# Half-size value pieces queued behind the steps of a recurrence, and one more value group moved among them

## The chip, the cores and the metric

The kernel runs on one core of a Trainium2 chip. The metric is the device time of one execution in microseconds (us), as the median of several runs. The engines named below are PE (TensorE, the matmul engine), DVE (VectorE), ACT (ScalarE), POOL (GpSimd) and SP (SyncE, which here issues nearly all transfers). A line number such as L516 is a line of the kernel before.

## The reference

A two-layer encoder trunk over 256 tokens of width 2048. Layer 0 mixes tokens by causal pooling, layer 1 by a recurrence (RWKV-7 style). Each mixer is followed by a gated feed-forward network of width 5632. What matters here is layer 1:

```
xr, xw, xk, xv, xa, xg = (h + xx * mu[j] for j in range(6))
r = xr @ w_r ;  k = xk @ w_k ;  v = xv @ w_v
g = sigmoid(xg @ g_la) @ g_lb
...
def step(state, inp):                    # per token, 32 heads of 64
    sa = einsum('bhvk,bhk->bhv', state, a_t)
    state = state * w_t + sa * b_t + v_t * k_t
    return state, einsum('bhvk,bhk->bhv', state, r_t)
...
return (normed(y) * g) @ w_o
```

The values `v` are a product of 256 x 2048 by 2048 x 2048, and each head needs only its own 64 columns of them.

## The kernel before, in words

Every float32 weight is split into a high and a low part (`split_weights`, L140): a transfer into a `raw` buffer, a cast on ACT into `wh` (L152), a subtraction on DVE into `wl` (L153). A product is then three matmuls. There are four `raw` buffers (`RAW`) and two each of `wh` and `wl` (`WB`).

The 2048 channels of layer 1 are worked in eight groups of 256 channels (four heads each). `values(gi)` (L504) makes the values of one group: four weight pieces of 512 KB, each with 24 matmuls of 256 columns (L515, L516, L517), 96 in all, accumulated in one PSUM bank and copied out by ACT (L520). Its left operands are the sixteen tiles `xv`, which are taken from a pool `mx` of forty tiles that other intermediates share.

The stages of layer 1 that matter follow each other like this:

- The values stage (L794): `values(0)` to `values(3)`, woven with the gate projections (`loras`, L711 to L713) and with `invert(0)`, a triangular inversion of small systems for groups 0 to 3, which is a long row of alternating products and sums on DVE (L633, L634). Its systems come back from DRAM (`dM`, L624) and its results go there (`dZ`, `dW`, L637, L639).
- A preparation stage (L1071): the first six of the sixteen remaining value pieces (`LV`), half of `prepare` for groups 4 to 7, and `ready(0)`, which loads one group's tiles (`KB`, `AR`, L832, L833), transposes them (L840), forms the gram tiles (L853, masked by DVE in L856) and completes the inverses (L875, L882).
- The recurrence (L1084): `all_chains()` advances the chains of the groups. A group's chain has twelve steps, four chunks of tokens with three products each (L907 and L910; L916; L921 and L925, then the state update on DVE in L930 or L932), with ACT copies between them (L912, L917, L937). A new group starts every eight steps (`STAG`), so one or two chains are alive, and there are 68 steps. Woven into these steps are the remaining ten value pieces (over steps 0 to 20, `VL`), the rest of `prepare`, `invert(1)`, `ready` of the later groups, `head_norm` with the gating (L958 to L960), and the output projection (`out_proj`, L1022 to L1024) from step 26 on.

The function `weave` (L432) only sets the order in which instructions are traced: after each step of its main generator, every other generator is advanced as far as it is due. The order on each engine is then made by a planner that simulates a timeline (L1162): it takes instructions as they become ready in the simulation, by priority, which is the traced order unless it is raised. The chain steps are raised by 30 (`HP`). A value matmul that is ready early can thus be placed long before the step it was traced in. `queued(name)` (L137) ties the instructions traced under it behind a recorded instruction on the same engine: they can be placed later than that one, not earlier. On the chip each engine works its list in order.

Of the kernel before, what the change touches and what calls it, by code (L numbers as in the profile page):

```python
# [10 lines left out]
F32 = mybir.dt.float32  # L11
# [24 lines left out]
HP, VL, HNL = 30, 20, 6  # L36
LV, LP, PE_, IE = 6, 14, 8, 16
# [55 lines left out]
def hybrid_encoder(ctx: ExitStack, tc: tile.TileContext, I, out):  # L93
# [156 lines left out]
    def ffn(layer, each=None):  # L250
        gcol = par[f"g2_{layer}"]
        with ExitStack() as st:
# [4 lines left out]
            rb = base[:, 4864:]  # L257
# [192 lines left out]
    def rwkv():  # L450
        with ExitStack() as st:
# [52 lines left out]
            def values(gi):  # L504
# [3 lines left out]
                for u in range(4):  # L508
                    (w, l), = split_weights(I["wv"][gi, u // 2][:, (u % 2) * 1024:(u % 2 + 1) * 1024])
                    for kk in range(4):  # L510
                        k = u * 4 + kk
                        cs = slice(kk * 256, (kk + 1) * 256)
                        for i in range(2):
                            xh, xl = xv[k][:, i * 128:(i + 1) * 128], xv[k][:, 256 + i * 128:256 + (i + 1) * 128]
                            nc.tensor.matmul(av[:, i], lhsT=xh, rhs=w[:, cs], start=(k == 0 and i == 0), stop=False, skip_group_check=True)  # L515
                            nc.tensor.matmul(av[:, i], lhsT=xh, rhs=l[:, cs], start=False, stop=False, skip_group_check=True)  # L516
                            nc.tensor.matmul(av[:, i], lhsT=xl, rhs=w[:, cs], start=False, stop=(k == 15), skip_group_check=True)  # L517
                    if u == 3:
                        vts[gi] = mx(F32, "vt") if gi < 4 else late[0].tile([128, 512], F32, name="vt", tag="vt", bufs=4)
                        nc.scalar.copy(vts[gi], acc)  # L520
                    yield
# [122 lines left out]
            with tc.tile_pool(name="rp1", bufs=1) as p1:  # L644
# [140 lines left out]
                for k in range(16):  # L785
# [8 lines left out]
                weave(chained(values(0), values(1), values(2), values(3)),  # L794
                      (loras(I["ga"], ("mu_g", "mu_g"), 128, (AF.Sigmoid, AF.Sigmoid), hid[2:]), 17, 0, 12),
                      (invert(0), 18, 0, 14))
# [90 lines left out]
            def chains(gi):  # L887
# [10 lines left out]
                for c in range(4):  # L898
# [5 lines left out]
                    with tc.high_priority(HP):  # L904
                        cb = cb_bank().rearrange("p (j x c) -> p j x c", j=2, x=2)
                        for jj, hc, u in heads_:
                            nc.tensor.matmul(cb[:, jj, 0, hc], lhsT=g_[jj][u % 2][k_, c], rhs=rows_of(u)[k_], start=(u == 0), stop=False, skip_group_check=True)  # L907
# [6 lines left out]
                    with tc.high_priority(HP):  # L914
                        for jj, hc, u in heads_:
                            nc.tensor.matmul(cb[b_, jj, 1, hc], lhsT=z[b_, u * 2 + i], rhs=rhs[b_, jj, hc], start=True, stop=True, skip_group_check=True)  # L916
                        nc.scalar.copy(two(vrow[b_]), cb[b_, :, 1])  # L917
                    yield
                    with tc.high_priority(HP):
                        for jj, hc, u in heads_:  # L920
                            nc.tensor.matmul(cb[k_, jj, 0, hc], lhsT=g_[jj][u % 2][b_, c, k_], rhs=rows_of(u)[b_], start=False, stop=True, skip_group_check=True)  # L921
# [244 lines left out]
```

## Time and profile before

| | us |
|---|---|
| median of 3 runs | 2184.95 |
| lowest and highest | 2180.51, 2186.39 |
| the profiled execution, its own time | 2181.9 |
| its span in the trace | 2180.1 |
| PE busy | 2116.9 (97% of the span) |
| DVE busy | 1553.9 (71%) |
| ACT busy | 1147.3 (53%) |
| mean granted PE clock | 0.981 |

The profile is one execution; times in it count from the span's start. "Busy" for PE counts overlapping, pipelined matmuls, so a full PE row does not mean that PE works at its peak. The granted clock is a share of full speed. In rows of stages the columns are the stage, its length, then for each engine the busy time with the number of instructions, then the granted clock, the mean busy share of the DMA engines and the GB/s that they moved. In rows of groups of instructions the last columns are the busy time, the mean duration in ns, and the idle time of the engine before them with what ended it. In rows of waits they are the total, the number of times and the longest. In rows of the timeline they are the start, the length, the engine and line, and in brackets the idle time before, with its releaser.

### The profile page before, as it was taken

How to read it: one execution, taken by the hardware profiler on the slowest of the kernel's cores; microseconds unless marked ns; L12 is line 12 of the kernel's file. 1: busy time of each engine (PE TensorE's matmuls, PEld its weight loads, DVE VectorE, ACT ScalarE, POOL GpSimd, SP SyncE). 2: the span in 40 equal slices, each digit the busy share in tenths (PEclk: the TensorE clock that was granted, in tenths of full speed). 3: DMA queues.
4: the chain of work that ended last, by engine and by line, in shares of the span. 5: the costliest groups of instructions: out<-in, count | busy, mean ns of one | idle time of the engine just before them, and what ended most of it. 6: DMA issues, size and time to landing. Idle time of an engine off the chain costs nothing.

```text
span 2180.1 us, 34748 instructions
## 1 busy us (share of the span) xinstructions
PE 2116.9 (97%) x13318; PEld 1843.5 (85%) x13318; DVE 1553.9 (71%) x2548; ACT 1147.3 (53%) x1884; POOL 30.6 (1%) x72
## 2 busy tenths in 40 slices
PE   7999999999999989999999999999999999999997
PEld 5888888888878879999988778788888888888786
DVE  8666666666787978688866767876666666677886
ACT  5544444444555478766745354554444444445444
POOL 0000000000000000011000000000000000000000
PEclk9999999999999999999998699999999999999999
DMA  6555565665566645466565343446666666655654
GB/s 232 174 187 191 186 191 187 190 187 190 196 198 217 207 155 163 163 210 207 171 218 151 108 121 105 160 121 191 188 189 189 188 189 189 188 191 199 204 202 156
DMA packets 147478, 395.11 MB, mean 181 GB/s; under 512 B 39280, under 2 KB 46832, under 8 KB 147056
## 3 DMA queue, kind: packets, MB, share of 16 engines
q1 hardware_dynamic: 146160, 390.80, 56.2%
q8 instruction: 104, 1.70, 0.3%
q10 hardware_dynamic: 1152, 2.10, 0.3%
q14 instruction: 62, 0.51, 0.1%
HBM read 376.59 MB, written 16.25 MB: 180 GB/s over the span
## 4 chain that ended last, share of the span: by engine, by line
PE 86%; DVE 6%; DMA 4%; ACT 2%; issue 1%; SPq 0%; ACTq 0%; DVEq 0%
PE acc L311 29%; PE acc L347 17%; PE acc L313 15%; PE acc L691 2%; PE acc L689 2%; PE acc L690 2%; DVE wl L153 2%; PE tp L347 2%; PE acc L1022 1%; PE acc L1024 1%; PE acc L1023 1%; DMA raw<-in_w 1%; PE acc L516 1%; PE acc L515 1%; PE cb L907 1%
## 5 line engine op out<-in xcount | busy, mean ns | idle before, releaser
L153 DVE TENSOR_TENSOR wl<-raw,wh 128x1024 fp32r<-128x1024 f32 (+1 forms) x525 | 640.2, 1220 | 432.2 <-ACT wh L152 428.0
L152 ACT CAST wh<-raw 128x1024 fp32r<-128x1024 f32 (+1 forms) x525 | 548.5, 1045 | 648.7 <-PE acc L311 276.9
L311 PE MATMUL acc<-xs,wh 128*128 128x512 f32 x2816 | 710.6, 393 | 3.7 <-DVE xs L266 3.2
L311 PEld LDWEIGHTS acc<-xs,wh 128*128 128x128 f32 x2816 | 504.9, 189 | 94.9 <-DVE xs L266 5.1
L313 PEld LDWEIGHTS acc<-xs,wl 128*128 128x128 f32 x2816 | 384.1, 190 | 27.5
L313 PE MATMUL acc<-xs,wl 128*128 128x256 f32 x2816 | 392.7, 282 | 0.0
L347 PE MATMUL acc<-vh,gT 128*128 128x512 f32 x640 | 184.9, 390 | 0.8 <-ACT vh L152 0.8
L347 PEld LDWEIGHTS acc<-vh,gT 128*128 128x128 f32 x640 | 119.7, 188 | 27.3 <-ACT vh L152 2.6
L691 PE MATMUL acc<-mx,wl 128*128 128x256 f32 x464 | 133.0, 287 | 3.5 <-DVE wl L153 3.5
L689 PE MATMUL acc<-mx,wh 128*128 128x256 f32 x464 | 132.1, 285 | 0.0
L690 PE MATMUL acc<-mx,wh 128*128 128x256 f32 x464 | 131.8, 284 | 0.0
L153 DVE TENSOR_TENSOR vl<-raw,vh 128x1024 fp32r<-128x1024 f32 x80 | 95.5, 1221 | 27.1 <-ACT vh L152 19.7
L347 PE MATMUL acc<-vl,gT 128*128 128x512 f32 x320 | 112.2, 389 | 0.0
L152 ACT CAST vh<-raw 128x1024 fp32r<-128x1024 f32 x80 | 80.9, 1050 | 49.3 <-PE acc L347 22.7
L355 ACT CAST vh<-T 128x1024 fp32r<-128x1024 f32 x56 | 58.9, 1052 | 80.5 <-DVE T L397 43.6
L347 PE MATMUL acc<-wh,gT 128*128 128x512 f32 x320 | 93.8, 390 | 0.7 <-ACT wh L152 0.7
L691 PEld LDWEIGHTS acc<-mx,wl 128*128 128x128 f32 x464 | 88.5, 191 | 5.3 <-DVE wl L153 5.2
L689 PEld LDWEIGHTS acc<-mx,wh 128*128 128x128 f32 x464 | 88.5, 191 | 0.8
L690 PEld LDWEIGHTS acc<-mx,wh 128*128 128x128 f32 x464 | 88.6, 191 | 0.0
L347 PE MATMUL acc<-vh,g 128*128 128x512 f32 x280 | 77.9, 391 | 1.1 <-ACT vh L355 0.6
L516 PE MATMUL acc<-wl,mx 128*128 128x256 f32 x256 | 74.2, 290 | 1.2 <-DVE wl L153 1.1
L515 PE MATMUL acc<-wh,mx 128*128 128x256 f32 x256 | 74.2, 290 | 0.0
(329 smaller groups left out, 3118.5 us busy)
## 6 DMA issues: line engine op xcount, KB each, us to landing
raw<-in_w SPq DMA_DIRECT2D x528, 512.0 KB, 4.4
raw<-in_wk SPq DMA_DIRECT2D x32, 512.0 KB, 3.7
raw<-in_wr SPq DMA_DIRECT2D x32, 512.0 KB, 3.7
raw<-in_wv SPq DMA_DIRECT2D x32, 512.0 KB, 4.0
raw<-in_wo SPq DMA_DIRECT2D x32, 512.0 KB, 3.6
raw<-in_pw SPq DMA_DIRECT2D x8, 512.0 KB, 7.8
dKB<-KB SPq DMA_DIRECT2D x16, 256.0 KB, 3.1
dKB<-AR SPq DMA_DIRECT2D x16, 256.0 KB, 3.7
```

The lines of the kernel that those rows point to most:

```text
L152: nc.scalar.copy(wh[:P, :step], raw[:P, :step])
L153: nc.vector.tensor_sub(wl[:P, :step], raw[:P, :step], wh[:P, :step].bitcast(F32))
L311: nc.tensor.matmul(acc, lhsT=w[:, cs], rhs=xs[q * 4 + kk], start=(q + kk == 0), stop=False, skip_group_check=True)
L313: nc.tensor.matmul(acc[:, :256], lhsT=l[:, cs], rhs=xs[q * 4 + kk][:, :256], start=False, stop=(q + kk == 6), skip_group_check=True)
L347: nc.tensor.matmul(out_, lhsT=lhsT, rhs=rhs, start=start, stop=stop, skip_group_check=True)
L355: nc.scalar.copy(wh, src)
L515: nc.tensor.matmul(av[:, i], lhsT=xh, rhs=w[:, cs], start=(k == 0 and i == 0), stop=False, skip_group_check=True)
L516: nc.tensor.matmul(av[:, i], lhsT=xh, rhs=l[:, cs], start=False, stop=False, skip_group_check=True)
L689: nc.tensor.matmul(acc[:, :256], lhsT=w[:, cs], rhs=xs[k][:, :256], start=(k == 0), stop=False)
L690: nc.tensor.matmul(acc[:, :256], lhsT=w[:, cs], rhs=xs[k][:, 256:], start=False, stop=False)
L691: nc.tensor.matmul(acc[:, :256], lhsT=l[:, cs], rhs=xs[k][:, :256], start=False, stop=(k == 15))
L907: nc.tensor.matmul(cb[:, jj, 0, hc], lhsT=g_[jj][u % 2][k_, c], rhs=rows_of(u)[k_], start=(u == 0), stop=False, skip_group_check=True)
```

## The change

- `values(gi)` hands back control after every second block of channels instead of every fourth: eight pieces of 12 matmuls a group instead of four of 24. The weight transfers and splits keep their size, one for two pieces.
- Once a chain has begun, the matmuls of each piece are traced under `queued("chain")`. The chain functions record each of their products of L907, L916 and L921 as `last["chain"]`, so a piece can't be placed ahead of the last such product of the step that it is traced behind.
- The values stage makes three groups (`VF = 3`) instead of four, and the gate projections and the inversion are due over 18 and 21 of its 24 half pieces (before: 12 and 14 of 16 pieces). The fourth group comes first among the remaining ones.
- Of the remaining 40 half pieces, 12 lie in the preparation stage (`LV`, one and a half groups as before) and 28 in steps 0 to 30 of the recurrence (before: 10 whole pieces in steps 0 to 20).
- `rb` names its 256 columns by both ends.

```
-HP, VL, HNL = 30, 20, 6
-LV, LP, PE_, IE = 6, 14, 8, 16
+HP, VL, HNL = 30, 30, 6
+VF, LV, LP, PE_, IE = 3, 12, 14, 8, 16
...
-            rb = base[:, 4864:]
+            rb = base[:, 4864:5120]
...
                     for kk in range(4):
                         k = u * 4 + kk
                         cs = slice(kk * 256, (kk + 1) * 256)
-                        for i in range(2):
-                            ... three matmuls
-                    if u == 3:
-                        vts[gi] = mx(F32, "vt") if gi < 4 else late[0].tile([128, 512], F32, name="vt", tag="vt", bufs=4)
-                        nc.scalar.copy(vts[gi], acc)
-                    yield
+                        with queued("chain") if "chain" in last else ExitStack():
+                            for i in range(2):
+                                ... the same three matmuls
+                        if k % 2 and k < 15:
+                            yield
+                vts[gi] = mx(F32, "vt") if gi < 4 else late[0].tile([128, 512], F32, name="vt", tag="vt", bufs=4)
+                nc.scalar.copy(vts[gi], acc)
+                yield
...
-                weave(chained(values(0), values(1), values(2), values(3)),
-                      (loras(I["ga"], ("mu_g", "mu_g"), 128, (AF.Sigmoid, AF.Sigmoid), hid[2:]), 17, 0, 12),
-                      (invert(0), 18, 0, 14))
+                weave(chained(*(values(g) for g in range(VF))),
+                      (loras(I["ga"], ("mu_g", "mu_g"), 128, (AF.Sigmoid, AF.Sigmoid), hid[2:]), 17, 0, 6 * VF),
+                      (invert(0), 18, 0, 7 * VF))
...
-                            nc.tensor.matmul(cb[:, jj, 0, hc], lhsT=g_[jj][u % 2][k_, c], ...
+                            last["chain"] = nc.tensor.matmul(cb[:, jj, 0, hc], lhsT=g_[jj][u % 2][k_, c], ...
...
-                            nc.tensor.matmul(cb[b_, jj, 1, hc], lhsT=z[b_, u * 2 + i], ...
+                            last["chain"] = nc.tensor.matmul(cb[b_, jj, 1, hc], lhsT=z[b_, u * 2 + i], ...
...
-                            nc.tensor.matmul(cb[k_, jj, 0, hc], lhsT=g_[jj][u % 2][b_, c, k_], ...
+                            last["chain"] = nc.tensor.matmul(cb[k_, jj, 0, hc], lhsT=g_[jj][u % 2][b_, c, k_], ...
...
-            vals = chained(*(values(g) for g in range(4, 8)))
+            vals = chained(*(values(g) for g in range(VF, 8)))
...
-            more += [(vals, 16 - LV, 0, VL), (prep, 28 - LP, 0, PE_), (invert(1), 18, PE_, IE), (reload(), 1, STAG + 12, STAG + 13)]
+            more += [(vals, 8 * (8 - VF) - LV, 0, VL), (prep, 28 - LP, 0, PE_), (invert(1), 18, PE_, IE), (reload(), 1, STAG + 12, STAG + 13)]
```

More of the change, by code (lines that the diff above doesn't have):

```diff
@@ L512, in values @@
                         cs = slice(kk * 256, (kk + 1) * 256)
-                        for i in range(2):
[L514 to L517, printed above, removed]
-                    if u == 3:
-                        vts[gi] = mx(F32, "vt") if gi < 4 else late[0].tile([128, 512], F32, name="vt", tag="vt", bufs=4)
-                        nc.scalar.copy(vts[gi], acc)
-                    yield
+                        with queued("chain") if "chain" in last else ExitStack():
+                            for i in range(2):
+                                xh, xl = xv[k][:, i * 128:(i + 1) * 128], xv[k][:, 256 + i * 128:256 + (i + 1) * 128]
+                                nc.tensor.matmul(av[:, i], lhsT=xh, rhs=w[:, cs], start=(k == 0 and i == 0), stop=False, skip_group_check=True)
+                                nc.tensor.matmul(av[:, i], lhsT=xh, rhs=l[:, cs], start=False, stop=False, skip_group_check=True)
+                                nc.tensor.matmul(av[:, i], lhsT=xl, rhs=w[:, cs], start=False, stop=(k == 15), skip_group_check=True)
+                        if k % 2 and k < 15:
[3 more added lines that the diff above has]
+                yield
             def placed(tile_, first):
@@ L906, in chains @@
                         for jj, hc, u in heads_:
-                            nc.tensor.matmul(cb[:, jj, 0, hc], lhsT=g_[jj][u % 2][k_, c], rhs=rows_of(u)[k_], start=(u == 0), stop=False, skip_group_check=True)
+                            last["chain"] = nc.tensor.matmul(cb[:, jj, 0, hc], lhsT=g_[jj][u % 2][k_, c], rhs=rows_of(u)[k_], start=(u == 0), stop=False, skip_group_check=True)
                         if c:
@@ L915, in chains @@
                         for jj, hc, u in heads_:
-                            nc.tensor.matmul(cb[b_, jj, 1, hc], lhsT=z[b_, u * 2 + i], rhs=rhs[b_, jj, hc], start=True, stop=True, skip_group_check=True)
+                            last["chain"] = nc.tensor.matmul(cb[b_, jj, 1, hc], lhsT=z[b_, u * 2 + i], rhs=rhs[b_, jj, hc], start=True, stop=True, skip_group_check=True)
                         nc.scalar.copy(two(vrow[b_]), cb[b_, :, 1])
@@ L920, in chains @@
                         for jj, hc, u in heads_:
-                            nc.tensor.matmul(cb[k_, jj, 0, hc], lhsT=g_[jj][u % 2][b_, c, k_], rhs=rows_of(u)[b_], start=False, stop=True, skip_group_check=True)
+                            last["chain"] = nc.tensor.matmul(cb[k_, jj, 0, hc], lhsT=g_[jj][u % 2][b_, c, k_], rhs=rows_of(u)[b_], start=False, stop=True, skip_group_check=True)
                         if c < 3:
```

## The prediction

> **What bounds the kernel now.** I read the page first: engine shares, and the clock by slices.
>
> ```profile
> span 2180.1 us, 34748 instructions
> ...
> PE 2116.9 (97%) x13318; PEld 1843.5 (85%) x13318; DVE 1553.9 (71%) x2548; ACT 1147.3 (53%) x1884; POOL 30.6 (1%) x72
> ...
> PEclk9999999999999999999998699999999999999999
> ```
>
> TensorE (PE) is busy almost throughout, at full granted clock but for one place: slices 21 and 22 (each 54.5 us) read 8 and 6. So I asked for busy time by stage around it: values with the gate projections (1020 to 1076), preparation (to 1111.5), the first recurrence steps with value work (to 1176), the steps after the value work is used up (to 1251.8), the rest of the recurrence (to 1411).
>
> ```profile
> core 0: us, PE busy (x) PEld busy (x) DVE busy (x) ACT busy (x) POOL busy (x), PEclk, DMA share, GB/s
> 1020.00:1076.00 56.00, 55.11 (x453) 54.29 (x453) 51.73 (x117) 35.65 (x67) 2.11 (x3) 1.00 0.52 165
> 1076.00:1111.50 35.50, 32.87 (x276) 30.86 (x276) 21.62 (x41) 22.41 (x41) 2.91 (x8) 0.95 0.74 228
> 1111.50:1176.00 64.50, 64.50 (x730) 58.01 (x728) 44.97 (x96) 35.30 (x78) 5.44 (x14) 1.00 0.56 182
> 1176.00:1251.80 75.80, 67.54 (x540) 56.30 (x541) 50.82 (x138) 28.74 (x68) 1.87 (x3) 0.66 0.40 116
> 1251.80:1411.00 159.20, 156.84 (x1403) 126.89 (x1402) 117.35 (x236) 81.53 (x171) 1.84 (x3) 0.98 0.40 126
> ```
>
> The first and third stages are limited by PE, with DVE close behind in the first (51.73 of 56). The fourth is the weak one: mean clock 0.66, and 75.80 - 67.54 = 8.3 us with no matmul at all. How the clock moves there is seen in windows of 2 us around each transition:
>
> ```profile
> 1182.00:1184.00 2.00, 1.91 (x18) 1.53 (x17) 0.00 (x0) 0.84 (x2) 0.00 (x0) 0.88 0.97 138
> ...
> 1216.00:1218.00 2.00, 2.00 (x7) 1.21 (x6) 1.86 (x5) 0.13 (x1) 0.76 (x1) 0.59 0.00 0
> ...
> 1234.00:1236.00 2.00, 1.78 (x13) 1.34 (x12) 1.23 (x2) 1.98 (x2) 0.00 (x0) 0.68 1.01 347
> ...
> 1250.00:1252.00 2.00, 2.00 (x6) 1.55 (x6) 0.33 (x1) 0.00 (x0) 0.00 (x0) 0.56 0.00 0
> ...
> 1282.00:1284.00 2.00, 0.96 (x5) 0.74 (x3) 1.66 (x4) 1.13 (x4) 0.00 (x0) 0.62 0.81 246
> ...
> 1288.00:1290.00 2.00, 2.00 (x11) 1.35 (x9) 0.69 (x1) 0.00 (x0) 0.00 (x0) 0.67 0.25 69
> ```
>
> Clocks are 1.00 or 0.50, so a mean gives the instant: 0.88 means a fall at 1183.5, 0.59 a rise at 1217.6, then fall 1234.7, rise 1251.8, fall 1282.5, rise 1289.3. The half-clock stretches last 34.1, 17.1 and 6.8 us. The first two, 51.2 us, cost up to 25.6 us of PE time; that is what is to be had.
>
> Where the value matmuls stand (one of their three lines, by the first three stages), and their spacing at full and, for the same shape in the gating, at half clock:
>
> ```profile
> 1020.00:1076.00 56.00, 33.72 (x118) 22.58 (x118) 1.00 0.52 165
> 1076.00:1111.50 35.50, 17.30 (x59) 11.45 (x58) 0.95 0.74 228
> 1111.50:1176.00 64.50, 23.23 (x80) 15.17 (x80) 1.00 0.56 182
> ...
> 1167.95 0.28 PE L517 MATMUL acc<-wh,mx 128*128 128x256 f32 x1
> ...
> 1169.14 0.28 PE L515 MATMUL acc<-wh,mx 128*128 128x256 f32 x1
> ...
> 1193.00 0.41 PE L960 MATMUL g<-hid,lbl 128*128 128x256 f32 x1
> ...
> 1194.92 0.41 PE L960 MATMUL g<-hid,lbl 128*128 128x256 f32 x1
> ...
> L516 PE MATMUL acc<-wl,mx x256: 274/283/415, 1020.6 to 1171.1; 128*128 128x256 f32 x128
> ```
>
> From 1167.95 to 1169.14 lie ten starts, 0.119 us each at full clock; from 1193.00 to 1194.92 nine, 0.213 us at half. With three lines, 3 x 80 = 240 value matmuls stand in the first recurrence stage; the last starts at 1171, so none is left for 1176 onward. Recurrence steps are dated by the chain's first product:
>
> ```profile
> L907 PE MATMUL cb<-vt,base x32: 214/272/320, 1111.6 to 1180.5; 64*128 64x64 f32 x32
> ...
> L907 PE MATMUL cb<-vt,G x96: 272/272/472, 1197.7 to 1385.3; 64*128 64x64 f32 x96
> ```
>
> Group 0 begins at 1111.6 (step 0); group 2, the first whose gram tiles are not in `base`, at 1197.7 (step 16): 86.1 / 16 = 5.4 us a step. The remaining 52 steps end about 1409, 4.1 us a step. So 1176 is step 12, and step 30 falls near 1255, just past the second half-clock stretch.
>
> **The change, part by part.** No arithmetic is added or removed: 768 value matmuls, 32 weight loads, 32 casts and 32 subtractions before and after. The edit of `rb` names the same 256 columns and costs nothing.
>
> *The fourth group leaves the values stage.* It is 96 matmuls, 96 x 0.119 = 11.4 us of PE, and four splits on DVE:
>
> ```profile
> L153 DVE TENSOR_TENSOR wl<-raw,wh 128x1024 fp32r<-128x1024 f32 x16 | 19.5, 1217 | 0.4 <-ACT wh L152 0.3
> ```
>
> 4 x 1.217 = 4.9 us. Since DVE stands at 51.73 of 56 with PE at 55.11, taking away 11.4 of PE and 4.9 of DVE leaves DVE first, near 47 of work. The inversion and gate projections are paced over 21 and 18 half pieces of 24, so their DVE work is packed, not cut. The saving lies between 4.9 (DVE) and 11.4 (PE); it is zero if the recurrence's start hangs on the transfers behind the inversion. I take 6, nearest to DVE.
>
> *The first steps hold fewer pieces.* A half piece is 12 matmuls, 1.43 us. By step 12, 13 of the 28 are due: 156 matmuls instead of 240. PE is busy 64.50 of 64.50 here, so 84 x 0.119 = 10.0 us come out, less where a chain's own latency shows instead. Bounds 0 and 10.0; I take 7, because PE is full throughout.
>
> *Steps 13 to 30 receive 15 pieces,* 180 matmuls: 21.4 us at full clock, 180 x 0.213 = 38.3 at half. There are 8.3 us of empty PE to absorb them, and the clock they may hold up. With s the share of the 51.2 us that is no longer at half clock, the stage changes by 38.3 - 16.9 s - 8.3 - 25.6 s = 30.0 - 42.5 s. Adding -6 and -7, the whole is 17.0 - 42.5 s, zero at s = 0.40.
>
> What s is depends on two falls. The first follows a stall that the change leaves:
>
> ```profile
> 1179.34 6.73 SPq L624 DMA_DIRECT2D sysM<-dM  x4
> ...
> DVE sysP L633 <- DMA sysM<-dM: 7.3, 1, 7.3
> ...
> PE cb L921 <- ACT sv L917: 4.0, 1, 4.0
> PE g L840 <- DMA KB<-dKB: 2.9, 3, 1.9
> ```
>
> DVE stands 7.3 us before the second inversion's first product, the head norms and state updates behind it wait, and PE runs dry for 4.0 us. Only the piece of the present step can fill that, so the first fall probably comes again. The rise is what I expect earlier. Compare the third stretch:
>
> ```profile
> 1283.16 0.80 PE L1022 MATMUL acc<-wh,ys 128*128 128x512 f32 x1 [1.04 <-DVE G L856]
> ...
> 1288.02 0.63 PE L1024 MATMUL acc<-wh,ys 128*128 128x512 f32 x1
> ```
>
> From 1283.16 on, full-width matmuls ran solid and the clock rose at 1289.3, two periods of 3.4 us after its fall; 3.4 us divides the other stretches too (10 and 5 times). In the first stretch such matmuls came only with the output projection. One piece at half clock is 12 x 0.213 = 2.6 us solid: alone a little short of a period, with gating or the next piece beside it enough. I take s = 0.65 in the first stretch and 0.8 in the second, whose fall came among chain products with little full-width work: (0.65 x 34.1 + 0.8 x 17.1) / 51.2 = 0.70. The sum is 17.0 - 29.8 = -12.8.
>
> The Trainium skill, "TensorE: Matmul & The Clock Gate", Part 1, puts this period at 3413 ns and has one busy period lift the clock; the trace agrees on the period. Its section "Why this matters for your kernels" asks for no idle gap above about 3 us. The second fall, with about 1 us idle before it, does not obey that: by that rule alone the second stretch would not be there, nor its 0.8 x 8.5 = 6.8 us to be won, and the sum would be -6.
>
> *Queues.* Value weights load on SP (0.33 us an issue); those behind the 6.73 us of L624 come late, and a late weight leaves its step's piece empty. Casts on ACT now wait for pieces that wait for chain steps, because only two `wh` buffers exist; behind such a cast stand the chain's copies. The nearest row:
>
> ```profile
> ACT wh L152 <- PE acc L1024: 4.9, 1, 4.9
> ```
>
> The DVE splits (7.5 x 1.217 = 9.1 us after 1176) fit beside 50.82 of 75.8. The sixteen `xv` tiles of the 40 `mx` stay until step 30 instead of 1171; a shortage would make the next group's KB loads late, and doubling today's 2.9 us of that wait costs 2.9. Two output-projection banks of three are wanted from step 26. For these I take zero, covered by the pieces themselves, with 4.9 + 2.9 = 7.8 as upper bound.
>
> The profiled execution took 2181.9 us (span 2180.1 and 1.8 around it), 3 below the median 2184.95. -12.8 gives 2169 against it and 2172 against the median; I say 2171.
>
> **Rivals.** *The moved work runs cold (slower).* The stall at 1180 drops the clock, and one piece a step never makes a solid period before the output projection does. Place: 1183 to 1217. Price: s = 0.2 gives 17.0 - 8.5 = +8.5, 2193; s = 0 gives +17, 2202. It decides below s = 0.40. For: the gating's twelve same-shaped matmuls from 1192.4 did not lift the clock, and PE records read nearly full there while it stayed 0.50. Against: a second such block in every step.
>
> *What leaves early is paid later (no change).* DVE and the inversion's transfers keep the start of the recurrence where it is (0 instead of -6), and at s = 0.55 the rest is -7 + 30.0 - 23.4 = -0.4: about 2183. For: DVE's 51.73 of 56. Against: the 4.9 us that DVE itself loses.
>
> *Nearly all is recovered (more gain).* Full PE savings, -11.4 - 10.0, and s = 0.9 give -21.4 + 30.0 - 38.2 = -29.6: about 2153. The first fall would have to vanish too; the 4.0 us gap speaks against it.
>
> *The order does not come out as written.* The queueing forbids a piece to go early, not late: if weights lag, pieces bunch at steps 20 to 30 beside the output projection, the first stretch stays cold and the second is cured, s = 17.1 / 51.2 = 0.33, +3.0, with 7.8 of queue waits +10.8: about 2195. Speaking for it: SP's 6.73 us.
>
> **How the numbers follow.** Forecast 0.50 (2160 to 2178); nearly all recovered 0.14; no change 0.18; cold 0.12; bunched 0.06. Runs of this kernel spread over 0.3%, so that is the bound for a difference. Faster 0.64, same 0.18, slower 0.18. The range 2151 to 2196 holds the recovered case's 2153 and reaches past the nearer slower ones, leaving out s = 0; it runs across both signs, but most of it is gain.
>
> **What would show it.** Value matmuls spread past 1230; the chain's first product some 5 us earlier than 1111.6; group 2's start about 13 us earlier than 1197.7 if the clock holds; one half-clock stretch below 15 us in place of 34.1, the second gone or short; PE-empty time in steps 13 to 30 below 8.3 us. Wrong, if the clock of these steps stays near 0.66 with 128x256 matmuls 0.21 us apart, if the values stage shortens by nothing, or if the chain's copies wait behind casts.

## The result, and the profile after

The changed kernel takes 2214.61 us (median of four runs, 2210.89 to 2217.57) against 2185.67 for the kernel before beside it: a ratio of 1.0134, with a 95% interval of 1.0109 to 1.0159. The forecast was 2171, so the sign was wrong. The profiled execution of the changed kernel has a span of 2209.1 us, 29.0 more than that of before. In its code the lines behind L515 stand one or two lower: the value matmuls are L516 to L518, the chain's first product is L909, the output projection L1024 to L1026.

First the page of the changed kernel:

```profile
span 2209.1 us, 34761 instructions
...
PE 2146.9 (97%) x13318; PEld 1866.5 (84%) x13318; DVE 1552.9 (70%) x2548; ACT 1147.1 (52%) x1884; POOL 29.4 (1%) x72
...
PEclk9999999999999999999868989999999999999999
```

The low clock is still there. Counted from 1, slices 20 to 22 and 24 read 8, 6, 8, 8, where before slices 22 and 23 read 8 and 6 (the prediction counts them from 0), so it begins two slices earlier. PE is "busy" 30 us longer with the same number of matmuls.

To see where the time went, both traces are cut at the same events: the last receptance product (before the values stage), the ends of groups 0, 2 and 6 (the square in `head_norm`, L980 before and L982 after; called here steps 12, 28 and 60, from which they are due; the first comes some 13 us behind the 1176 that the prediction calls step 12), and FFN 1's first matmul. Busy time by stage, the kernel before:

```profile
1019.80:1189.30 169.50, 162.07 (x1545) 151.48 (x1543) 122.89 (x263) 96.91 (x194) 11.57 (x27) 0.97 0.60 188
1189.30:1259.40 70.10, 65.75 (x549) 54.55 (x550) 51.67 (x134) 29.53 (x68) 1.37 (x2) 0.68 0.31 94
1259.40:1385.10 125.70, 123.85 (x1144) 100.34 (x1142) 87.59 (x174) 62.75 (x136) 1.23 (x2) 0.97 0.37 115
1385.10:1434.80 49.70, 47.19 (x260) 37.33 (x259) 44.32 (x95) 25.05 (x51) 0.00 (x0) 1.00 0.48 154
```

and the changed kernel:

```profile
1021.60:1192.00 170.40, 159.65 (x1331) 147.68 (x1330) 115.87 (x261) 86.79 (x184) 9.24 (x27) 0.80 0.52 161
1192.00:1263.10 71.10, 71.10 (x690) 61.60 (x691) 54.07 (x130) 35.41 (x73) 2.45 (x2) 0.97 0.43 135
1263.10:1415.20 152.10, 152.10 (x1229) 120.81 (x1225) 93.33 (x182) 67.57 (x142) 1.23 (x2) 0.94 0.36 111
1415.20:1464.70 49.50, 45.77 (x252) 37.48 (x251) 42.45 (x93) 24.76 (x52) 0.00 (x0) 0.97 0.43 135
```

The two stages up to step 28 together are only 1.9 us longer. In this pair of executions the whole loss, 26.4 us, stands in the third stage, in which no value matmul was to be moved. One of the three value lines in the first three of these stages, and one of the three output-projection lines in the last three; for each kernel the value rows come first:

```profile
1019.80:1189.30 169.50, 74.24 (x256) 0.97 0.60 188
...
1189.30:1259.40 70.10, 7.08 (x12) 0.68 0.31 94
1259.40:1385.10 125.70, 27.78 (x64) 0.97 0.37 115
1385.10:1434.80 49.70, 14.34 (x36) 1.00 0.48 154
```

```profile
1021.60:1192.00 170.40, 59.04 (x193) 0.80 0.52 161
1192.00:1263.10 71.10, 18.41 (x60) 0.97 0.43 135
1263.10:1415.20 152.10, 1.23 (x4) 0.94 0.36 111
...
1192.00:1263.10 71.10, 1.57 (x4) 0.97 0.43 135
1263.10:1415.20 152.10, 32.08 (x76) 0.94 0.36 111
1415.20:1464.70 49.50, 12.43 (x32) 0.97 0.43 135
```

From these rows comes a balance. The clock's loss is length times (1 - clock). A value matmul counts 0.119 us as in the prediction; one of the output projection counts 0.235, by four starts in the changed kernel's timeline, (1300.58 - 1299.64) / 4:

```profile
1299.64 0.39 PE L1026 MATMUL acc<-wh,ys 128*128 128x512 f32 x1
...
1300.58 0.39 PE L1024 MATMUL acc<-wh,ys 128*128 128x512 f32 x1
```

What is left over is called gaps: round trips, hand-overs, and the few small products that fall on the other side of a cut. The clock stands in the rows with two places, so the columns of clock and gaps hold to about 1 us. The balance says where the time stands, not what caused it.

| after minus before, us | length | clock's loss | values | output projection | gaps |
|---|---|---|---|---|---|
| to step 12 | +0.9 | +29.0 | -22.5 (-189) | 0 | -5.6 |
| steps 12 to 28 | +1.0 | -20.3 | +21.4 (+180) | -5.6 (-24) | +5.5 |
| steps 28 to 60 | +26.4 | +5.3 | +1.4 (+12) | +8.5 (+36) | +11.2 |
| to FFN 1 | -0.2 | +1.5 | 0 | -2.8 (-12) | +1.1 |
| sum | +28.1 | +15.5 | 0.3 | 0.1 | +12.2 |

The moved values were absorbed between steps 12 and 28, as forecast. Against the forecast, the place that they left got no shorter, and its clock fell; and the steps behind 28 got longer, where the output projection, which now starts 43 us later, stands with more gaps around it.

The first fall is seen in the changed kernel's timeline at the end of the preparation stage, and in windows of 2 and 20 us:

```profile
1087.93 0.28 PE L518 MATMUL acc<-wh,mx 128*128 128x256 f32 x1
1092.48 1.11 PE L842 MATMUL g<-base,KB 128*128 128x128 f32 x4 [4.27 <-DMA KB<-dKB]
```

```profile
1090.00:1092.00 2.00, 0.00 (x0) 0.00 (x0) 2.00 (x4) 0.73 (x2) 0.12 (x2) 0.73 0.76 182
...
1120.00:1140.00 20.00, 19.49 (x131) 17.29 (x132) 11.23 (x26) 9.48 (x24) 1.22 (x6) 0.50 0.47 155
```

PE ran out of value work at 1088 and waited 4.27 us for `KB`. The clock fell at 1090.9 (a mean of 0.73 in the first window) and, by the changes of the clock in the trace, came back at 1145.5: 54.6 us at half speed. In the kernel before the same wait was shorter, and value matmuls followed it at once:

```profile
1102.17 1.09 PE L840 MATMUL g<-base,KB 128*128 128x128 f32 x4 [2.37 <-DMA KB<-dKB]
1102.91 0.56 PE L515 MATMUL acc<-wh,mx 128*128 128x256 f32 x1
```

There the clock was down for 3.4 us.

### The profile page after: what moved, and what is told of

It reads as the page before. It is cut to its first block, busy times and chain, and to the rows that moved or that the text cites. A ratio compares the mean times of both kernels' runs of the same rounds, so it can differ in the third digit from the quotient of the medians.

```text
span 2209.1 us, 34761 instructions
## 1 busy us (share of the span) xinstructions
PE 2146.9 (97%) x13318; PEld 1866.5 (84%) x13318; DVE 1552.9 (70%) x2548; ACT 1147.1 (52%) x1884; POOL 29.4 (1%) x72
## 5 line engine op out<-in xcount | busy, mean ns | idle before, releaser
L516 PE MATMUL acc<-wh,mx 128*128 128x256 f32 x256 | 78.7, 307 | 0.0
```

## The experiments

Each ratio is to the kernel before on the same chip in the same job (its medians lay between 2179 and 2182 us there), with its 95% interval. The ratios are taken from all runs of a job; the ratio of the two medians can differ from them by up to 0.0024.

**The parts of the change.** The changed kernel without the queue:

```
-                        with queued("chain") if "chain" in last else ExitStack():
+                        with ExitStack():
```

> The changed kernel without the queueing alone: half pieces, three groups in the values stage, 28 pieces over 30 steps stay. Theory S (the queueing starves the start: value matmuls can no longer fill the wait for the KB transfers and the first steps, so the clock falls to half at 1091 and stays there for 54.6 us): the value matmuls run ahead again, the half-clock stretch at the start is gone or below 10 us, the time comes back to 2178 to 2192. Theory G (moving the fourth group costs, whatever the order on PE): it stays above 2205. Theory R (any new order made by the planner shifts the half-clock stretches by chance): anywhere between 2170 and 2215, with stretches in other places.

Measured: 2192.09 us, 1.0048 [1.0025, 1.0072]. Without the queue the planner pulls the values forward again (the last one at 1166 instead of 1265), the long fall at 1091 is gone, and some 19 of the 29 us with it; the time lies 0.1 us above the range of theory S and far below that of theory G.

The changed kernel with four groups in the values stage:

```
-VF, LV, LP, PE_, IE = 3, 12, 14, 8, 16
+VF, LV, LP, PE_, IE = 4, 12, 14, 8, 16
```

> The changed kernel with four groups in the values stage again (20 half pieces over 30 steps instead of 28), queueing and half size stay. Theory S: five and a half groups stand before the recurrence as in the kernel before, so the wait for the first KB transfer is filled and the fall at 1091 does not come at that place; the first steps still get one piece each, so part of the loss stays: 2190 to 2205, half-clock time before the feed-forward network between 61 and 92 us. Theory G: back to 2180 to 2188. Theory R: no order in it.

Measured: 2196.87 us, 1.0080 [1.0056, 1.0104], as theory S had it. In place of the long fall at 1091 stands one of 3.4 us at 1097, but up to step 12 there are still 51 us of half clock in all.

The queue alone, added to the kernel before with its whole pieces, four groups and twenty steps (the line that is added; the chain's products are recorded as in the change):

```
+                        with queued("chain") if "chain" in last else ExitStack():
```

> The kernel before with the queueing alone: whole pieces, four groups in the values stage, 10 pieces over 20 steps, each behind its chain step. Theory S: slower than before, 2190 to 2210, with more half-clock time in the steps 0 to 12 than the kernel before (3.4 us there). Theory G: within 0.3% of before, 2179 to 2192.

Measured: 2194.70 us, 1.0074 [1.0043, 1.0105], again as theory S had it. Its stage to step 12 and the next:

```profile
1020.90:1190.40 169.50, 162.62 (x1411) 152.38 (x1410) 119.91 (x267) 91.44 (x188) 10.08 (x27) 0.87 0.55 174
1190.40:1258.30 67.90, 67.90 (x635) 56.84 (x634) 50.61 (x125) 32.93 (x70) 1.56 (x2) 0.92 0.38 121
```

The first has 134 matmuls fewer than before (1411 against 1545) and lasts exactly as long, at a clock of 0.87 instead of 0.97.

The changed kernel with 20 instead of 12 half pieces ahead of the recurrence:

```
-VF, LV, LP, PE_, IE = 3, 12, 14, 8, 16
+VF, LV, LP, PE_, IE = 3, 20, 14, 8, 16
```

> The changed kernel with 20 half pieces in the preparation stage, not queued, instead of 12, and 20 over the 30 steps instead of 28; three groups in the values stage stay. Theory S: the unqueued pieces fill the wait for the KB transfers, the first fall goes or comes later, 2185 to 2203. Theory G: no better than the changed kernel, above 2208.

Measured: 2189.22 us, 1.0045 [1.0024, 1.0066], in theory S's range.

Half pieces alone (e5: the changed kernel without the queue, with four groups and twenty steps), and the moved group alone (e6: as e5, but three groups and whole pieces, with the pacing numbers for whole pieces):

```
-HP, VL, HNL = 30, 30, 6
-VF, LV, LP, PE_, IE = 3, 12, 14, 8, 16
+HP, VL, HNL = 30, 20, 6
+VF, LV, LP, PE_, IE = 4, 12, 14, 8, 16        (e6: 3, 6, 14, 8, 16)
...
-                        with queued("chain") if "chain" in last else ExitStack():
+                        with ExitStack():
...
-                        if k % 2 and k < 15:           (e6 alone)
+                        if k % 4 == 3 and k < 15:      (e6 alone)
```

> The kernel before with the half size alone: four groups in the values stage, 20 half pieces over steps 0 to 20, no queueing. Theory S (the queueing and the moved group starve the seam before the recurrence and its first steps): no difference, 0.997 to 1.003 of before. Rival R (every new order of the planner costs up to 10 us by chance): anywhere from 0.995 to 1.006.

> The kernel before with the move of the fourth group alone: three groups in the values stage, 14 whole pieces over steps 0 to 20 after the six of the preparation, no queueing. Theory S: the unqueued pieces run ahead into the values stage, so the fourth group still ends near 1081 and the inversion's store stays near 1075; nothing is won there; one group fewer stands at the wait for the KB transfers, so 1.002 to 1.008, as with half pieces and no queue (1.0048). Theory G (the move as such does harm by packing the inversion and the gate projections): the inversion's store later than 1080 and 1.006 or more. Rival by my prediction's step: 6 us saved before the recurrence, 0.997.

Measured: 2191.61 us, 1.0035 [1.0010, 1.0060], and 2206.99 us, 1.0128 [1.0079, 1.0177]. Both lie above theory S. The moved group alone costs as much as the whole change, though its values end at 1171.7 and its output projection begins at 1216.3, about as early as before; theory G foresaw the price but not the place, as the inversion's store goes out at 1077.1. The first experiment holds the same move, in half pieces over 30 steps, for 0.0048. So 0.0128 can't be the price of the move as such, and no run explains it.

Only the last group of values held back, by the queue over steps 11 to 19; the others are half pieces without a queue, as in e5 (only the parts of the lines that change):

```
-                        with queued("chain") if "chain" in last else ExitStack():
+                        with queued("chain") if held else ExitStack():
...
-(vals, 8 * (8 - VF) - LV, 0, VL)
+(vals, 8 * (7 - VF) - LV, 0, 12), (values(7, True), 8, 11, 19)
```

> A version between both: four groups in the values stage, groups 4 to 6 unqueued in half pieces up to step 12, and only the last group's 8 half pieces held behind their steps, 11 to 19, where the kernel before stands at half clock. Theory S: start of the recurrence as before, no fall before 1160; the eight pieces meet the wait for the second inversion: 0.993 to 1.002. If it is above 1.004, holding value matmuls back costs even where they are wanted, and the loss is not only in the starved start.

Measured: 2193.57 us, 1.0064 [1.0045, 1.0084], above the 1.004 from which, by the expectation, holding pieces back costs even where they are wanted. No part is free, and the parts do not add up: queue, half pieces and moved group alone give 0.0074 + 0.0035 + 0.0128 = 0.0237, and together 0.0134. So either each of them meets the same limit, or part of each number is only that the order was planned anew. The second was tested next.

**What a new layout costs.** The kernel before with one pacing number changed, in three ways, and the changed kernel with the same three edits:

```
-HP, VL, HNL = 30, 20, 6              (e9: 7, e13: 5; in the changed kernel e11: 7, e15: 5)
-LV, LP, PE_, IE = 6, 14, 8, 16       (e14: LP 15; in the changed kernel e16: LP 15)
```

> The kernel before with one pacing number changed (HNL, the steps over which head_norm with its gating is spread, 7 for 6): the same instructions, but the planner lays out a new order, in which some 400 rows of PE's list stand elsewhere. Theory A, the loss of the change lies in what it does to the values: a new layout alone costs nothing, 2179 us, between 2172 and 2186. Rival, any new layout of this tuned order costs: the half-steps tried so far (no queue, half pieces alone, last group alone) all cost 8 to 14 us, so this one would cost about 10 as well, 2189.

> The changed kernel with the same number changed (HNL 7 for 6). Theory A: the loss stays, since the fall of the clock at 1091 comes before head_norm first runs: 2208 to 2216 us, some 29 above the kernel before. Rival, the loss is an accident of one layout: a new one gives back 10 or more, 2204 or less.

> The kernel before with HNL 5 for 6 (head_norm and gating over five steps, the output projection due one step earlier): the same instructions in a new layout. Theory, the layout of before is a good one among many and any other costs about 9 us, nearly all of it behind step 28: 2186 to 2194 us. Rival, only the later pacing of HNL 7 cost that, and the earlier one costs nothing: 2176 to 2182.

> The kernel before with one more of the 28 preparation steps in the preparation stage (LP 15 for 14): a second new layout, changed in another place, ahead of the recurrence. Theory, any new layout costs about 9 us, behind step 28: 2186 to 2194 us. Rival, a change ahead of the recurrence costs nothing: 2176 to 2182.

> The changed kernel with HNL 5 for 6. Theory, of the 29 us about 9 are the price of a new layout, which the kernel before does not pay, and about 18 belong to the change in any layout: layouts of the changed kernel scatter around 2205, this one between 2196 and 2214. Rival, all 29 are the change's own and the other layouts were lucky: 2208 to 2216.

> The changed kernel with LP 15 for 14, the edit that cost the kernel before nothing measurable. Theory, the change's own part is about 20 us in any layout: between 2196 and 2214 us. Rival, layouts of the changed kernel scatter down to the kernel before's own time: 2192 or less.

The last two columns are stage lengths of the profiled execution: up to step 28, and from there to FFN 1, the tail.

| edit | kernel before, us | ratio | changed kernel, us | ratio | before: to 28, tail | changed: to 28, tail |
|---|---|---|---|---|---|---|
| none | 2179 to 2182 | 1 | 2214.61 | 1.0134 [1.0109, 1.0159] | 240, 175 | 241, 202 |
| HNL 7 | 2190.78 | 1.0042 [1.0025, 1.0059] | 2204.38 | 1.0091 [1.0055, 1.0126] | 237, 192 | 237, 191 |
| HNL 5 | 2187.99 | 1.0033 [1.0018, 1.0047] | 2206.26 | 1.0118 [1.0083, 1.0152] | 237, 189 | 243, 195 |
| LP 15 | 2181.93 | 1.0007 [0.9985, 1.0029] | 2212.31 | 1.0143 [1.0097, 1.0189] | 229, 187 | 246, 200 |

Two of three neutral edits cost 7 and 9 us, one nothing that can be measured. So neither statement holds as it was written: a new layout doesn't always cost 9 us, and it is not free. The three edits average 1.0027, the four layouts of the changed kernel 1.0122. Their difference, 0.0095 or about 21 us, is the better estimate of what the change itself does; some 6 to 8 of the 29 us are what almost any edit of this kernel risks.

The last columns change the picture that the first pair of profiles gave. The kernel before has the shortest tail of its own four layouts. Averaged over four layouts each, the change costs some 11 us in the tail and some 6 us up to step 28, not 26 and 2.

Where HNL 7 lost its 9 us is seen in its stages (to step 12, to 28, to 60):

```profile
1020.60:1188.40 167.80, 162.31 (x1525) 151.72 (x1523) 122.71 (x263) 96.67 (x195) 10.10 (x27) 0.98 0.60 190
1188.40:1257.70 69.30, 66.26 (x536) 53.13 (x535) 52.35 (x134) 29.18 (x65) 1.35 (x2) 0.68 0.33 96
1257.70:1397.80 140.10, 140.08 (x1180) 113.55 (x1180) 87.45 (x175) 63.20 (x139) 1.17 (x2) 0.90 0.33 107
```

The first two are 2.5 us shorter than before, the third 14.4 longer, of which 0.10 x 140.1 - 0.03 x 125.7 = 10.2 is clock. The kernel before lost only 3.8 us of clock there.

**What the falls of the clock are worth.** Spare matmuls of 128x256 whose bank nobody reads, in the changed kernel: 96 ahead of the recurrence and 12 in each of its first eight steps (e7), or 40 ahead of it (e12); in the kernel before: 30 behind step 12 (e10).

```
+            def spare(n, steps):
+                for step in range(steps):
+                    acc = acc_bank()
+                    with queued("chain") if "chain" in last else ExitStack():
+                        for q in range(n):
+                            nc.tensor.matmul(acc[:, :256], lhsT=xv[q % 16][:, :128], ...
+                    yield
```

> The changed kernel with 192 spare matmuls (128x256, operands that are there already, results never read): 96 unqueued between the preparation stage and the recurrence, and 12 behind each of the steps 0 to 7. They are 192 x 0.12 = 23 us more of PE work at full clock, and change nothing in the output. Theory S (the loss is half clock for lack of dense work at the start): the 54.6 us stretch at the start shrinks below 20 us, half-clock time before the feed-forward network falls from 92 to 70 us or less, and the 23 us of extra work are paid by it: ratio to before 1.008 to 1.016, no worse than the changed kernel (1.0134) by more than 0.003. Theory W (the time is PE work and hand-overs, the clock only follows): all of it but some 7 us of waits is added, 1.018 to 1.025.

> The changed kernel with 40 spare matmuls of 128x256 (their bank is not read; the output is unchanged) traced at the end of the preparation stage, 4.8 us of PE at 0.119 us each, of which 29 stand ahead of the first product that waits for KB: they fill some 3.5 of its 4.27 us. Theory, the half clock from 1090.9 to 1145.5 comes from this one gap and is worth half its length: the stretch vanishes, 27.3 us less for at most 4.8 of work, 2186 to 2192 against 2214. Rival, the first steps wait for their own round trips and not for PE's speed, so that the stretch costs little: the clock is up, the time falls by 8 at most, 2206 or more.

> The kernel before with 30 spare matmuls of 128x256 (their bank is not read; the output is unchanged) queued behind step 12 of the recurrence, 3.6 us of PE, where PE ran dry at 1180 with sysM late. Theory, the half clock from 1183.5 to 1217.6 is worth half its length and this fills its gap: up to 17 us less, less 0 to 3.6 for the work: 2164 to 2170 us against 2179. Rival, the gap is longer than the spare work or the stretch hides behind DVE: nothing is gained and the work may show, 2179 to 2183.

Measured: e7 2209.38 us, 1.0115 [1.0081, 1.0148]; e12 2194.38 us, 1.0065 [1.0040, 1.0090]; e10 2192.81 us, 1.0058 [1.0036, 1.0081]. The stages of e7 to step 12 and 28, and then the first of e12:

```profile
1018.70:1184.70 166.00, 163.09 (x1535) 152.14 (x1535) 117.90 (x266) 87.69 (x185) 10.53 (x27) 0.98 0.53 167
1184.70:1261.50 76.80, 76.80 (x680) 65.75 (x679) 51.80 (x125) 34.82 (x72) 1.90 (x2) 0.87 0.40 122
```

```profile
1023.00:1188.80 165.80, 157.69 (x1360) 147.30 (x1361) 112.76 (x250) 87.10 (x185) 9.93 (x27) 0.85 0.52 165
```

With 192 more matmuls, 192 x 0.119 = 22.8 us of work, the stage to step 12 is 4.4 us shorter than in the changed kernel: the clock is 0.98 instead of 0.80, which gives back 34.1 - 3.3 = 30.8 us. So work that seemed to be saved had been what kept the clock up. But the stage can't be shortened much by a full clock either: over all kernels here whose stages are shown it lasts 164 to 171 us, at clocks of 0.80 to 0.99 and with 1331 to 1545 matmuls. The chain shows the same: from the first product of group 0 to its square it takes 77.7 us in the kernel before, 94.0 in the changed one and 87.2 in e7. So a full clock with 22.8 us of added work gives back 7 of the 16 us; what paces the rest no run shows. e12 fits neither expectation: its ratio is 0.0069, some 15 us, below that of the changed kernel, and in the profiled executions 4.6 us of the difference stand in the stage where the spares are (they cut the wait of 4.27 us to 0.23, but the clock fell 10 us later, in the next wait for `KB`, of 4.01 us, and stands at 0.85), and 13.7 behind step 28, in a new layout. e10 missed both of its expectations too: it shortened the stalled steps 12 to 28 of the kernel before from 70.1 to 65.6 us and lost 16 behind step 28, as other layouts of it did; it was not a gain.

**Why the steps behind 28 got longer.** The kernel before with only the first round of the output projection made late, the values untouched:

```
-                        for j in (a, a + 1):
+                        with queued("chain") if pairs[0] == 0 else ExitStack():
+                         for j in (a, a + 1):
...
-                    more.append((out_proj(range(2 * first, 2 * g + 2)), 4 * count, at + OA, ...
+                    more.append((out_proj(range(2 * first, 2 * g + 2)), 4 * count, at + (4 if first == 0 else 0), ...
```

> The kernel before with the first round of the output projection (96 matmuls of 128x512 in eight pieces) due four steps later and queued behind the chain, the values as before. Theory, the steps up to 28 take the same time whatever PE does in them, so what is kept out of them is paid behind: with 20 to 34 of these matmuls displaced, 20 x 0.231 = 4.6 to 34 x 0.231 = 7.9 us more work behind step 28, on top of about 9 for the new layout: 2191 to 2197 us, and the steps up to 28 within 5 us of the 239.5 of before. Rival, the recurrence's start gets shorter by what is taken out of it: the first 28 steps lose 5 us or more, and the whole is no slower than another layout, 2182 to 2189.

Measured: 2208.59 us, 1.0115 [1.0082, 1.0149], 12 us above the theory's range and further above the rival's. Its stages, and one line of the output projection in the second and third:

```profile
1022.20:1186.50 164.30, 160.78 (x1523) 150.25 (x1522) 123.20 (x264) 97.07 (x195) 11.21 (x27) 0.99 0.60 193
1186.50:1261.80 75.30, 73.05 (x508) 62.60 (x508) 47.06 (x127) 26.78 (x64) 1.42 (x2) 0.50 0.29 84
1261.80:1411.90 150.10, 150.10 (x1200) 119.99 (x1199) 91.30 (x180) 65.51 (x140) 1.22 (x2) 0.91 0.32 99
1411.90:1468.30 56.40, 51.50 (x271) 40.66 (x270) 45.55 (x95) 24.36 (x50) 0.00 (x0) 0.94 0.41 136
...
1186.50:1261.80 75.30, 2.05 (x3) 0.50 0.29 84
1261.80:1411.90 150.10, 32.63 (x73) 0.91 0.32 99
```

The steps up to 28 take 164.3 + 75.3 = 239.6 us, as before, although the second stage ran at half clock from end to end (0.50). What was kept out of it, (12 - 3) x 3 = 27 matmuls or 6.3 us, came back behind step 28, with gaps and clock on top: 150.1 + 56.4 = 206.5 us against 175.4, 31.1 more. This one displacement, without touching a value, makes the tail as long as the whole change does (201.6). The profiled execution is the slowest of four, 6 us above their median, and a new layout's price is in it.

Then the reverse, the changed kernel with its queued pieces over 20 steps:

```
-HP, VL, HNL = 30, 30, 6
+HP, VL, HNL = 30, 20, 6
```

> The changed kernel with the 28 queued half pieces spread over 20 steps instead of 30 (VL 20 for 30); three groups in the values stage, half pieces and the queue stay. The values are then all placed ahead of the output projection's third weight piece, and at the 64th first product of the chains 54 of its matmuls are placed: 48 in the kernel before, 24 in the changed one, 12 in the one with the late output projection. Theory, the late output projection is what the change pays: with its pace restored about 17 of the 29 us come back and a layout's price is left, 2182 to 2194 us. Rival, the queue and the moved group cost by themselves (more small hand-overs on PE behind the chain): 2202 or more.

Measured: 2205.19 us, 1.0104 [1.0069, 1.0138]. The theory's time was missed; the rival's 2202 or more holds it. Its stages, and one line of the output projection in the second:

```profile
1021.70:1189.70 168.00, 158.46 (x1367) 146.83 (x1367) 115.33 (x256) 88.82 (x187) 8.60 (x27) 0.85 0.55 170
1189.70:1274.20 84.50, 84.50 (x703) 70.56 (x703) 59.51 (x142) 36.89 (x75) 1.95 (x3) 0.90 0.37 115
1274.20:1406.90 132.70, 132.70 (x1167) 107.18 (x1167) 87.49 (x175) 62.32 (x136) 0.61 (x1) 0.96 0.35 113
1406.90:1459.00 52.10, 47.92 (x259) 37.42 (x258) 43.03 (x93) 25.34 (x53) 0.00 (x0) 1.00 0.41 138
...
1189.70:1274.20 84.50, 6.65 (x15) 0.90 0.37 115
```

With the output projection back at its pace, the tail is 184.8 us instead of 201.6: 16.8 of its 26 us are recovered. But the steps 12 to 28 take 84.5 us instead of 71.1. That the two kinds of work don't fit there together is not shown by it: they hold 133 value matmuls and 45 of the output projection, 26.4 us, against 180 and 12, 24.2 us, in the changed kernel, and 6.3 of the 13.4 us more are clock.

The tails of all twenty kernels bear the theory out in its direction, not in its full size. In eleven of them 30 or more matmuls of the output projection stand between steps 12 and 28, and their tails are 175 to 194 us, 186.0 on average; in nine only 8 to 15 stand there, and the tails are 187 to 207, 197.5 on average. So a late output projection goes with some 11 us, and the rest of the 26 comes of comparing with one of the two shortest tails. No kernel here beat the kernel before.

## Why the prediction was wrong, step by step

- **"The fourth group leaves the values stage" (-6): failed.** It hardly left. The pieces of the preparation stage are traced before any chain exists, so the queue does not bind them, and the planner pulled them forward. One value line in the old stage's window, and in the remainder up to the chain's start, in the changed kernel:

```profile
1020.00:1076.00 56.00, 31.27 (x111) 1.00 0.53 164
1076.00:1098.00 22.00, 9.44 (x34) 0.84 0.78 223
```

  111 stand there instead of 118, where three groups alone would be 96: (118 - 111) x 3 x 0.119 = 2.5 us left instead of 11.4. The inversion's store, which the step wanted earlier, went out later (1075.37 before):

```profile
1079.71 0.33 SPq L639 DMA_DIRECT2D dZ<-sysZ  x1
```

- **"The first steps hold fewer pieces" (-7): failed.** The argument was that PE is busy 64.50 of 64.50. That count includes latency and overlapping matmuls, and says nothing of how much of it can be taken out. The queue alone took 134 matmuls out of the stage to step 12 and left its length at 169.5 us. In the changed kernel 22.5 us of matmuls went out and the length grew by 0.9, while the clock cost 29.0 more. The chain did start earlier (1098.0 against 1111.6), by more than the 5 us named as a sign; group 0 ended no earlier for it (1192.0 and 1189.3), and group 2 began at 1200.8 instead of 1197.7, where the prediction named a start about 13 us earlier as its sign.

- **A cost that was not in the sum: the clock of the stage that is emptied.** The working priced falls only where the trace already showed them, and took the first stages' clock of 1.00 and 0.95 as given. The value matmuls were the cover there, and no price was put on that cover being gone. The wait for `KB` appears in the prediction only as 2.9 us doubled by a shortage of tiles; as a wait of 4.27 us with nothing behind it, it began a stretch of 54.6 us of half clock. The gap alone did not make the stretch: with it filled (e12) the half clock up to step 12 still came to 51 us of 68.

- **"30.0 - 42.5 s" with s = 0.70, +0.25: right in size, by luck.** Steps 12 to 28 grew by 1.0 us with 180 value matmuls more, the very number forecast, though for a stage that was cut 13 us earlier. The clock recovered further than forecast: the loss of 22.4 us fell to 2.1, which is s = 0.91 and would have given -8.7. The empty time of PE is gone (71.10 busy of 71.10), but it was not gained: gaps grew by 5.5, while 5.6 of output projection went elsewhere. The first fall was expected to come again and be short; it was (10.2 and 3.4 us, from 1172.8 and 1189.9, by the changes of the clock in the trace). But the prediction's reason for it doesn't fit the order of time. In the kernel before the clock fell at 1183.5, and PE's stall of 4.0 us, which the prediction puts ahead of the fall, came behind it, from 1186.3 on; the longest idle time in the 7 us ahead of the fall is 0.79 us:

```profile
1190.29 1.11 PE L921 MATMUL cb<-sv,base 64*64 64x64 f32 x8 [4.01 <-ACT sv L917]
```

- **"Two output-projection banks of three are wanted from step 26. For these I take zero, covered by the pieces themselves": failed, and by most.** The price was given as at most 7.8 with the queue waits; what followed behind step 28 was 26.4 us, some 11 of them by the comparison over layouts. The output projection is traced from step 26 on, but in the kernel before the planner ran it from 1211.5. Now it begins near where the values end (1264.8); that it stands behind their banks and split buffers is the likely reason, which no run took apart. One of its lines, in the kernel before and in the changed one:

```profile
L1022 PE MATMUL acc<-wh,ys x112: 387/397/797, 1211.5 to 1425.5; 128*128 128x512 f32 x112
```

```profile
L1024 PE MATMUL acc<-wh,ys x112: 387/394/793, 1254.3 to 1455.7; 128*128 128x512 f32 x112
```

  Behind step 28, PE has nothing to spare, so 36 more of its matmuls are 8.5 us longer, and the gaps between kinds of work add 11.2. Moving work into a hole meant moving out what had been in the hole. Making the output projection late alone lengthened the tail by 31 us, more than the 12 to 17 that the neutral edits of that kernel add; bringing it back took 16.8 off, no more than a layout can do; the average over all kernels says some 11. So the direction is shown and the size is not, and why the gaps grow is not settled.

- **The rivals.** The slower ones had the sign, not the mechanism: the pieces moved behind step 12 did not run cold (only the first ones, up to 1145.5, did), and the pieces did not bunch at steps 20 to 30. "What leaves early is paid later" came nearest. Its kernel of truth is that the time to step 28 is not set by PE's load, and it failed in what it took the rest to be, since it looked for the payment in the same steps.

- **The size of the bound.** The forecast's range assumed that an edit is judged by its own terms. Two of three neutral edits of this kernel cost 7 and 9 us; no term stood for that.

What stays open: in every layout of the changed kernel and with the late output projection, the tail is longer than in the kernel before, but so it is in the three neutral layouts of that kernel. No run here separates the shape of the order (more changes between small and large matmuls) from when the work comes.

## What to carry to other kernels

Before pricing work that leaves a stage, ask whether that work kept the clock up or covered a wait there: a stage whose length PE's load does not set doesn't get shorter when matmuls are taken out of it, and its clock can fall. Before filling a hole, list what stands in the hole already and what is queued behind the filler's buffers, and see whether the place where that ends up has room. And where a planner lays out the order anew for any edit, run two or three neutral edits first: they show how large a difference has to be before it belongs to the edit.

## What the runs showed of the hardware

**Time splits into a steady part and a clock part.** Each run comes with its time and its mean granted clock. Time x clock is steady: in 25 runs of the kernel before it lies between 2137.1 and 2146.2 us, while the times go from 2170.6 to 2192.2. In the four runs of the changed kernel it is 2155.8 to 2159.9. So most of the spread between runs of one kernel is clock, 30 to 55 us of loss for the kernel before, and a change of a few us in the work shows sooner in this product than in the time. By the averages (2157.9 against 2141.9) the change costs about 16 us of granted time; the clock's loss is 56.5 against 38.2 us, some 18, while 29 less 16 would leave 13 (the runs of the two kernels come from different jobs here).

**A stage can be almost busy and stay cold.** From 1120 to 1140 in the changed kernel PE is busy 19.49 of 20 us and the clock stays at 0.50. These are 131 matmuls: some 94 small products of the inverse completion, the gram tiles and the chain, and between them 37 of 256 columns, for the values and the preparation, which at 0.213 us each, the spacing at half clock, fill 7.9 of the 20 us. The Trainium skill, "TensorE: Matmul & The Clock Gate", Part 1, has one busy window of about 3.4 us lift the clock. The lengths of the stretches agree (3.4, 6.8, 10.2, 13.7, 54.6 us, all multiples of 3.41), but what the profile counts as busy is not what that rule counts: cut back from the rise at 1145.5 into sixteen windows of 3.41 us, nine before the last one are counted busy throughout and did not lift it. Nor does a fall need idle time that the profile shows: steps 12 to 28 of the changed kernel are busy 71.10 of 71.10 us, and the clock fell in them, at 1237.7.

**In one place hand-overs between shapes of matmuls cost about 0.1 us each.** From the timeline of the changed kernel, behind step 28, where products of the inverse completion (32x32) and the chain's first products alternate:

```profile
1302.87 1.10 PE L909 MATMUL cb<-sv,G 64*128 64x64 f32 x8
1303.90 0.71 PE L912 MATMUL cb<-S,AR 128*128 128x128 f32 x4
...
1308.83 0.43 PE L909 MATMUL cb<-vt,G 64*128 64x64 f32 x2
1309.19 0.24 PE L877 MATMUL g<-w,m 32*32 32x32 f32 x2
1309.36 0.43 PE L909 MATMUL cb<-vt,G 64*128 64x64 f32 x2
```

Eight of L909 in one run take 1303.90 - 1302.87 = 1.03 us, 0.13 each. Two of them and two of L877 between take 1309.36 - 1308.83 = 0.53, where 2 x 0.13 and two of the far smaller ones, some 0.05, would be 0.31: two hand-overs cost 0.22. The clock is 1.00 in these windows. Counted through the timeline of steps 28 to 60, hand-overs between products of 32x32 and of 64x128 number 1 in the kernel before, some 40 in the changed one and some 30 with the late output projection and with the values over 20 steps. At this price they would be some 4 of the 11 us that the gaps grew by in the changed kernel. They are no general cause: in the changed kernel with HNL 5 they number 7, and its tail is 195 us.
